# A two-layer decoder trunk on one core: the late modulation columns move from TensorE matmuls to VectorE dots

## The chip, the cores and the metric

The kernel runs on one core of a Trainium2 chip. The metric is the device time of one execution in microseconds (us). Three runs of the kernel before gave 1697.27, 1698.01 and 1699.43 us; their median, 1698.01 us, is the time that the change is measured against.

## The reference, cut to what matters

A trunk of two layers on `x` (1 x 1024 positions x 1024 channels, float32). Each layer computes

```
mod = c @ mod_w[layer] + mod_b[layer]          # c: 1 x 1024, mod_w[layer]: 1024 x 3072
shift, scale, gate = the three thirds of mod
h = rms_norm(x, norm_w[layer]) * (1 + scale) + shift
x = x + gate * mixer(h)
```

The mixer of layer 0 projects `h` to 2560 channels, which feed a causal convolution (with a layer norm behind it) and a state-space recurrence (with a GLU behind it), and projects the two branches back. The mixer of layer 1 is attention with rotary positions. The change concerns how 32 of the 48 blocks of 128 values of `mod` are computed: the gate of layer 0 and all of layer 1. Shift and scale of layer 0 are needed at once and are computed ahead of this stage by other code that stays as it is. The rest are the late columns.

## The kernel before, in words

Channels lie on the 128 partitions, positions on the free axis. A float32 product is made from three matmuls (high x high, low x high, high x low; `mm3`, lines 231 to 233), so every weight is split into a high and a low part: the high part on ScalarE (ACT, line 209), the low part on VectorE (DVE, line 212).

Layer 0 (`layer0`) is an order written out by hand: the order of the instructions on TensorE (PE), VectorE, ScalarE and, from the projections on, GpSimd (POOL) is that of the program. Only the order on SyncE (SP), which issues every DMA, is left to the scheduler. The loop that matters runs over half projections, t = 0 to 41: output block t // 2, position half t % 2, 24 matmuls of 128x512 each (12 for the GLU, t = 26 to 33). A step t puts into the queues, in this order: what takes the result of step t-1 out of PSUM (`evac`), at even t the split of the next weight (`begin`), the side work hung on this step with `at(t, ...)`, then `mod_turn` and `mod_step`, and last the matmuls of the half projection (names `p`, `pg`).

The side work is: the rotary angles (`rope_tables`, at step 1, 14 VectorE instructions of 128x512 on tiles `ro`, two ScalarE sines, two DMAs to DRAM); four quarters of the recurrence (`ssm_quarter`, quarter j at steps 4j+2 to 4j+11: tiles `pk`, `kp`, `pgt`, `T`, `sr`, `si`, `V`, `W`, `X`, `py`); four convolutions (`conv`, steps 4j+8 to 4j+12: `cm`, `pc`); the layer norm of the convolution in two halves b (`ln_sum`, `ln_mean`, `ln_center`, `ln_var`, `ln_rsqrt`, `ln_norm` at steps 27 + 4b to 31 + 4b: `mu`, `lq`, `va`). From step 42 the output projections follow (`o...` for positions of half 0, `p...` of half 1, tiles `poo`, `pop`), and beside those of half 1, at steps 57 to 60, `hidden(k)` makes the input of layer 1, two blocks k a step: `x` (line 217, VectorE), its high part (line 218, ScalarE), its low part on VectorE for even k (line 224) and on GpSimd for odd k (lines 226 and 227). At step 60 `open_slabs` puts the splits of layer 1's first four weights (`fr`) behind them on ScalarE and GpSimd.

The late columns are computed by `mod_rows` (lines 251 to 276), one generator step per half projection at t = 4 to 25, 27, 31, 34 to 41 and once behind the loop. The first of these steps issues three loads; each of the other 32 multiplies two of 64 chunks. A chunk is 128 input channels x 512 output columns of `mod_w` (`in_mod_r`, 256 KB), in three buffers (two in tile `mw`, one in the tile `cb`); four matmuls of 32 columns by 128 (line 272, tile `pr`) take the vector c, repeated over 32 columns, against it, and behind them the load into the same buffer is issued (line 259). Every eighth chunk ends a group of four blocks: ScalarE copies the rows (line 275), and in the next step `mod_turn` (lines 278 to 292) turns them into a column with one matmul (line 286, tile `mc`) and adds the bias on VectorE (line 288).

The dot that the change uses exists already: `dot_c` (line 238), used for the early scale columns, multiplies a tile by c, spread over all partitions in `cb`, and sums along the free axis.

PSUM has eight banks: tag `ps` 3 (half projections, `mc`), `pm` 2 (everything of the quarters and the layer norm), `pr` 1, `pc` 2.

Of the kernel before, what the change touches and what calls it, by code (L numbers as in the profile page):

```python
# [64 lines left out]

MODR = ((0, 16), (0, 20), (1, 8), (1, 12), (1, 0), (1, 4), (1, 16), (1, 20))


class Trunk:
# [180 lines left out]

    def mod_rows(self, ps, pr):

        nc = self.nc
        w = self.u("mw", tag="mw").rearrange("p (i m n) -> p i m n", i=2, m=4)
        w = [w[:, 0], w[:, 1], self.cb[:, 512:1024].rearrange("p (m n) -> p m n", m=4)]

        def load(c):
            if c < 8 * len(MODR):
                nc.sync.dma_start(w[c % 3], self.I["mod_r"][c // 8, c % 8])

        for c in range(3):
            load(c)
        crep = self.cb[:, 0:256].rearrange("p (k n) -> p k n", k=8)
        rows = self.cb[:, 256:384]
        p = pr("pr")[:, 0:128]
        for n, (layer, m) in enumerate(MODR):
            for q in range(4):
                yield
                for k in (2 * q, 2 * q + 1):
                    c = 8 * n + k  # L270
                    for j in range(4):
                        nc.tensor.matmul(p[32 * j:32 * j + 32], lhsT=crep[:, k], rhs=w[c % 3][:, j], start=(k == 0),
                                         stop=(k == 7), tile_position=(0, 32 * j))
                    load(c + 3)
            nc.scalar.activation(rows, p, AF.Copy)
            self.mod_late = (ps, rows, layer, m)

    def mod_turn(self):

        if self.mod_late is None:  # L280
            return
        ps, rows, layer, m = self.mod_late
        self.mod_late = None
        nc = self.nc
        c = ps(f"mc{layer}{m}")[:, 0:4]
        nc.tensor.matmul(c, lhsT=rows, rhs=self.ident[:, 0::32], start=True, stop=True)
        t = self.consts.tile([128, 4], F32, name=f"mod{layer}_{m}")
        nc.vector.tensor_tensor(t, c, self.mod_bias(layer, m, 4), op=ALU.add)
        self.mod[layer][m:m + 4] = [t[:, j:j + 1] for j in range(4)]
        if layer and 8 <= m < 16:  # L290
            nw = _cols()["norm_w"][0] + layer * 8 + m - 8
            nc.vector.scalar_tensor_tensor(self.g1[:, m - 8:m - 4], t, 1.0, self.pk[:, nw:nw + 4], ALU.add, ALU.mult)


    def layer0(self):
        nc, tc, I = self.nc, self.tc, self.I
        with self.cx0 as cx:
# [6 lines left out]
            def ps(name, shape=None, tag="ps"):  # L304
                return pp.tile(shape or [128, 512], F32, tag=tag, name=name, bufs={"ps": 3, "pm": 2}[tag])

            def pm(name, shape=None):
                return ps(name, shape, "pm")

            def pr(name):  # L310
                return pp.tile([128, 512], F32, tag="pr", name=name, bufs=1)

# [36 lines left out]
            with tc.tile_pool(name="start", bufs=8) as sp, order:  # L349
# [21 lines left out]
                def fetch_m(m):  # L371
                    mw[m] = sp.tile([128, 1024], F32, tag="m", name=f"mw0_{m}")
                    nc.sync.dma_start(mw[m], I["scale0"][m - 8] if m > 7 else I["shift0"][m])

# [77 lines left out]
                sh = pc("sh")  # L452
                pu, place = self.ssm_u_psum(ps, pm, pr)
                for k in range(8):
# [37 lines left out]
            nc.vector.tensor_copy(self.cb[:, 0:256].rearrange("p (k n) -> p k n", k=8),  # L492
                                  self.ccol.unsqueeze(2).to_broadcast([128, 8, 32]))
            cx.enter_context(tc.manual_schedule(engines={mybir.EngineType.DVE, mybir.EngineType.Activation,
# [37 lines left out]
            short = lambda a: a.rearrange("p (t c) -> p t c", t=8)  # L532
            mods = [None]
            self.mod_late = None

            def mod_step():
                if mods[0] is None:
                    mods[0] = self.mod_rows(ps, pr)
                next(mods[0], None)

# [7 lines left out]
            conv = [None] * 4  # L548
            at(1, self.rope_tables)
            for j in range(4):  # L550
# [66 lines left out]
            for b in range(2):  # L617
                at(25, ln_sum, b)
                t = 27 + 4 * b
                at(t, ln_mean, b)  # L620
                at(t, ln_center, b, 0)
                at(t + 1, ln_center, b, 1)
                at(t + 3, ln_var, b)
                at(t + 3, ln_rsqrt, b)
                at(t + 4, ln_norm, b, (0, 1, 2, 3))

# [67 lines left out]
            for t in range(42):  # L694
                i, h = divmod(t, 2)
                key = seq[i]
                if done:
                    evac(*done)
                if h == 0:
                    begin(i)  # L700
                for fn in side.pop(t, ()):
                    fn()
                self.mod_turn()
                if 4 <= t < 26 or t in (27, 31) or t > 33:
                    mod_step()
# [10 lines left out]
            mod_step()  # L716

# [36 lines left out]
            def hidden(k):  # L754
                h = self.h1[k][0] = self.u(f"h1_{k}_0", F32R, [128, 2, 512])
                self.affine(h[:, 0], h[:, 1], x0[k // 2][:, k % 2], self.g[1][k], st["r"], self.mod[1][k],
                            ("vector", "gpsimd")[k % 2])

# [5 lines left out]
            for k in range(8):  # L764
                at(57 + k // 2, hidden, k)
            at(60, open_slabs)
            done, po = None, {}
            for i in range(21, len(seq)):
                t, key = i + 21, seq[i]
                m, b = int(key[1]), int(key[0] == "p")  # L770
                if done:
                    residual(*done)
                    done = None
                begin(i)
                for fn in side.pop(t, ()):
                    fn()
                self.mod_turn()
# [12 lines left out]
                if key == "p0":  # L790
                    stat()
# [64 lines left out]
    def rope_tables(self):  # L856
        nc = self.nc
        xn = self.u("ro", shape=[128, 2, 8, 64], tag="mw")
        x, n = xn[:, 0], xn[:, 1]
# [651 lines left out]

    def ssm_u_psum(self, ps, pm, pr):
        p = {(j, h): (ps, ps, ps, pm, pm, pr)[2 * j + h](f"pu{j}_{h}") for j in range(3) for h in range(2)}
        mm = self.nc.tensor.matmul
# [23 lines left out]
    def ssm_quarter(self, j, us, ps, ysg):  # L1538
# [147 lines left out]
def lay_out(inp):  # L1686
    a = {k: np.asarray(v) for k, v in inp.items()}
    f = np.float32
# [8 lines left out]
    def put(name, v):  # L1697
# [51 lines left out]
        "ident": np.eye(128, dtype=f),  # L1749
        "scale0": a["mod_w"][0].T.reshape(24, 128, 1024)[8:16],  # L1750
        "mod_r": np.stack([a["mod_w"][i][:, 128 * m:128 * m + 512].reshape(8, 128, 512) for i, m in MODR]),
        "w0": tl(a["even_w_in"][0]).reshape(20, 128, 1024),
# [30 lines left out]
```

## Time and profile before

| | before |
|---|---|
| three runs, us | 1697.27, 1698.01, 1699.43 (median 1698.01) |
| the profiled execution, us | 1702.04 |
| its span, first to last instruction, us | 1700.3 |
| mean granted TensorE clock | 0.991 |
| TensorE busy | 1663.6 us (98%) |
| VectorE busy | 952.2 us (56%) |
| ScalarE busy | 618.9 us (36%) |
| GpSimd busy | 514.6 us (30%) |

Times in the rows are us from the start of the span unless they are marked ns. A matmul of float32 stands in the records as two, so `x8` are four instructions. The granted clock is a share of 2.4 GHz: 0.50 is 1.2 GHz. "Idle before, releaser" is the time that an engine sat still ahead of an instruction, and what ended it.

### The profile page before, as it was taken

The numbers are of one execution on the slowest core, as the hardware profiler recorded it, in microseconds if no ns is written. First come the engines' busy times: TensorE is split into PE (matmuls) and PEld (weight loads), VectorE is DVE, ScalarE is ACT, GpSimd is POOL, SyncE is SP. The second block draws the span as 40 slices with busy tenths as digits, with TensorE's granted clock in tenths as the row PEclk, the third lists the DMA queues.
The fourth block names the chain that finished last, engine by engine and source line by source line (L and its number), as shares of the span: only waits on it lengthen the run. The fifth ranks groups of instructions, "written<-read, shape, count | busy, mean of one in ns | idle before, by whom it ended". The sixth has DMA issues, their size and how long they took to land.

```text
span 1700.3 us, 28611 instructions
## 1 busy us (share of the span) xinstructions
PE 1663.6 (98%) x10520; PEld 1516.7 (89%) x10520; DVE 952.2 (56%) x2336; ACT 618.9 (36%) x1860; POOL 514.6 (30%) x733
## 2 busy tenths in 40 slices
PE   8989999999989999999999999999999999999999
PEld 5877777677769999999999999999999999999887
DVE  8964543545567446645654754754664575565541
ACT  5333333634344343333433334333333343333410
POOL 6454401000155323332332431432333233333000
PEclk9999999999989999999999999999999999999999
DMA  9355555346532012112112211211211211111252
GB/s 348 135 177 174 166 167 183 119 129 194 170 100 64 25 57 76 44 29 73 51 35 62 80 35 49 80 38 51 81 45 29 72 54 38 48 63 63 88 172 95
DMA packets 94189, 159.84 MB, mean 94 GB/s; under 512 B 13281, under 2 KB 43745, under 8 KB 94050
## 3 DMA queue, kind: packets, MB, share of 16 engines
q1 hardware_dynamic: 94050, 158.02, 30.0%
q8 instruction: 83, 1.36, 0.3%
q14 instruction: 56, 0.46, 0.1%
HBM read 130.54 MB, written 23.23 MB: 90 GB/s over the span
## 4 chain that ended last, share of the span: by engine, by line
PE 83%; issue 5%; DVE 4%; DMA 3%; ACT 2%; SPq 2%; POOL 1%; ACTq 0%; DVEq 0%; POOLq 0%
PE pj L231 17%; PE pj L233 17%; PE pj L232 17%; PE O L1149 4%; PE S L1100 4%; PE p L231 3%; PE p L232 3%; PE p L233 3%; PE tqk L1054 2%; PE tP L1127 2%; PE po L233 2%; PE po L232 2%; PE po L231 2%; DMA mw<-in_mod_r 1%; SPq L1669 1%
## 5 line engine op out<-in xcount | busy, mean ns | idle before, releaser
L231 PE MATMUL pj<-wh,h 128*128 128x384 f32 x1536 | 542.9, 353 | 0.0
L233 PE MATMUL pj<-wh,h 128*128 128x384 f32 x1536 | 516.7, 336 | 0.7 <-DVE h L224 0.7
L232 PE MATMUL pj<-wl,h 128*128 128x384 f32 x1536 | 516.0, 336 | 0.0
L231 PEld LDWEIGHTS pj<-wh,h 128*128 128x128 f32 x1536 | 289.1, 188 | 1.0 <-issue 0.2
L232 PEld LDWEIGHTS pj<-wl,h 128*128 128x128 f32 x1536 | 289.7, 189 | 0.3 <-issue 0.2
L233 PEld LDWEIGHTS pj<-wh,h 128*128 128x128 f32 x1536 | 288.3, 188 | 1.3 <-DVE h L224 1.3
L1039 POOL TENSOR_TENSOR B<-u,sin 128x256 f32<-128x256 f32 x192 | 190.1, 990 | 209.1 <-DVE u L1035 209.1
L1011 ACT ACTIVATE sq<-pj 128x128 f32<-128x128 f32 x384 | 103.0, 274 | 351.4 <-PE pj L233 317.9
L1012 POOL TENSOR_SCALAR ss<-ss 128x2 f32<-128x2 f32 x192 | 40.8, 212 | 488.4 <-ACT sq L1011 488.2
L212 DVE TENSOR_TENSOR wl<-raw,wh 128x768 fp32r<-128x768 f32 (+1 forms) x124 | 116.0, 950 | 124.2 <-ACT wh L209 123.6
L1035 DVE SCALAR_TENSOR_TENSOR u<-pj,ss,pk 128x128 f32<-128x128 f32 x384 | 116.4, 345 | 74.4 <-POOL ss L1013 74.2
L1076 DVE COPY qk<-tqk 128x256 f32<-128x256 f32 x188 | 79.2, 421 | 139.6 <-PE tqk L1054 139.6
L1013 POOL TENSOR_TENSOR ss<-ss,mh 128x2 f32<-128x2 f32 x192 | 139.1, 724 | 16.0
L1120 ACT ACTIVATE E<-E,nm 128x256 f32<-128x256 f32 (+2 forms) x128 | 71.3, 557 | 198.6 <-DVE nm L1119 198.6
L231 PE MATMUL p<-h0h,wh 128*128 128x512 f32 x272 | 113.1, 416 | 0.0
L233 PE MATMUL p<-h0h,wl 128*128 128x512 f32 x272 | 109.4, 402 | 0.0
L232 PE MATMUL p<-h0l,wh 128*128 128x512 f32 x272 | 109.3, 402 | 0.0
L209 ACT ACTIVATE wh<-raw 128x768 fp32r<-128x768 f32 (+1 forms) x124 | 97.3, 790 | 29.1 <-PE po L232 14.2
L1047 DVE TENSOR_TENSOR u<-A,B 128x128 f32<-128x128 f32 x192 | 56.2, 293 | 88.1 <-POOL B L1039 81.3
L1046 DVE TENSOR_TENSOR A<-u,cos 128x256 f32<-128x256 f32 x192 | 96.8, 504 | 4.4
L1100 PE MATMUL S<-qk 128*128 128x128 f32 x544 | 86.4, 274 | 0.0
L1100 PEld LDWEIGHTS S<-qk 128*128 128x128 f32 x544 | 80.9, 190 | 1.4
(452 smaller groups left out, 2797.3 us busy)
## 6 DMA issues: line engine op xcount, KB each, us to landing
raw<-in_wqkv SPq DMA_DIRECT2D x92, 384.0 KB
mw<-in_mod_r SPq DMA_DIRECT2D x43, 256.0 KB
wr<-in_w SPq DMA_DIRECT2D x17, 512.0 KB
al<-ad SPq DMA_DIRECT2D x16, 512.0 KB
cb<-in_mod_r SPq DMA_DIRECT2D x21, 256.0 KB
x<-in_x SPq DMA_DIRECT2D x8, 512.0 KB
mw<-in_scale SPq DMA_DIRECT2D x8, 512.0 KB
mw<-in_shift SPq DMA_DIRECT2D x8, 512.0 KB
```

Of the source, the lines that this page charges most:

```text
L209: nc.scalar.activation(hi, src, AF.Copy)
L212: getattr(nc, leng).tensor_tensor(lo, src, hi.bitcast(F32), op=ALU.subtract)
L231: mm(ps, lhsT=lh, rhs=rh, start=first, stop=False)
L232: mm(ps, lhsT=lh, rhs=rl, start=False, stop=False)
L233: mm(ps, lhsT=ll, rhs=rh, start=False, stop=last)
L1011: sc.activation(sq[:, i], p[:, i * 128:(i + 1) * 128], AF.Square, accum_out=ss[:, i:i + 1])
L1013: gp.tensor_tensor(ss, ss, mh, op=ALU.pow)
L1035: v.scalar_tensor_tensor(u[:, i].rearrange("p a b -> p (a b)"), p[:, i * 128:(i + 1) * 128], ss[:, i:i + 1], w, ALU.mult, ALU.mult)
L1039: gp.tensor_tensor(f(B), f(u), sin[:, ti].unsqueeze(1).to_broadcast([128, 4, 64]), op=ALU.mult)
L1046: v.tensor_tensor(f(A), f(u), cos[:, ti].unsqueeze(1).to_broadcast([128, 4, 64]), op=ALU.mult)
L1076: v.tensor_copy(out, tp)
L1100: pe.matmul(ps[:, i * 128:(i + 1) * 128], lhsT=qT[h, g, t], rhs=kT[h, g, kt], start=True, stop=True)
```

## The change

- `mod_rows` and `mod_turn` go, with the tile `pr`, its PSUM bank, the repeated c and the input `mod_r`. `mod_dots` comes: 64 dots, each over 128 output channels x 512 input channels of `mod_w` transposed (256 KB, 128 rows of 2 KB), behind each a load into its buffer (three buffers: two in `mw`, a new `mx`). Every eighth dot is followed by two adds of 128x4 (and for the scale of layer 1 one more instruction, as before).
- Two dots are put behind the matmuls of a half projection, at t = 4 to 26, 30 and 34 to 41. The first three loads are issued ahead of the loop.
- The rotary angles move from step 1 to step 20, into tiles of the pool `e`.
- The freed PSUM bank goes to `pm` (3 now). The tile `T` of the recurrence has one buffer instead of two.
- Layer norm: half 1 starts at step 30 instead of 31; the variance of half 0 comes at step 31 and its norm at 32 instead of 30 and 31. Variance and norm of half 1 stay at 34 and 35.
- `hidden(k)`: low parts on VectorE for all k, at steps 57, 58, 58, 59, 60, 60, 61, 62 instead of two each at 57 to 60.

```diff
-    def mod_rows(self, ps, pr):
...
-                for k in (2 * q, 2 * q + 1):
-                    c = 8 * n + k
-                    for j in range(4):
-                        nc.tensor.matmul(p[32 * j:32 * j + 32], lhsT=crep[:, k], rhs=w[c % 3][:, j], start=(k == 0),
-                                         stop=(k == 7), tile_position=(0, 32 * j))
-                    load(c + 3)
-            nc.scalar.activation(rows, p, AF.Copy)
...
+    def mod_dots(self):
...
+        w = self.u("mw", tag="mw")
+        w = [w[:, 0:512], w[:, 512:1024], self.c0.tile([128, 512], F32, name="mx")]
+        halves = [(layer, m, i) for layer, m0 in MODS for m in range(m0, m0 + 4) for i in range(2)]
...
+                nc.sync.dma_start(w[n % 3], self.I["mod_w"][layer, m][:, 512 * i:512 * i + 512])
+        for n in range(3):
+            load(n)
+        for n, (layer, m, i) in enumerate(halves):
+            yield
...
+            self.dot_c(h[:, n % 8 // 2, i:i + 1], w[n % 3], slice(512 * i, 512 * i + 512))
+            load(n + 3)
+            if n % 8 == 7:
...
+                nc.vector.tensor_tensor(t, h[:, :, 0], h[:, :, 1], op=ALU.add)
+                nc.vector.tensor_tensor(t, t, self.mod_bias(layer, m, 4), op=ALU.add)
...
-            at(1, self.rope_tables)
+            at(20, self.rope_tables)
...
-                t = 27 + 4 * b
+                t = 27 + 3 * b
...
-                at(t + 3, ln_var, b)
-                at(t + 3, ln_rsqrt, b)
-                at(t + 4, ln_norm, b, (0, 1, 2, 3))
+                at(t + 4, ln_var, b)
+                at(t + 4, ln_rsqrt, b)
+                at(t + 5, ln_norm, b, (0, 1, 2, 3))
...
-                self.mod_turn()
-                if 4 <= t < 26 or t in (27, 31) or t > 33:
-                    mod_step()
                 p = ps(f"p{key}_{h}")
...
                 done = (key, h, p)
+                if 4 <= t < 27 or t == 30 or t > 33:
+                    mod_step(2)
...
-                at(57 + k // 2, hidden, k)
+                at((57, 58, 58, 59, 60, 60, 61, 62)[k], hidden, k)
...
-        T = L(f"T{j}", "T", [128, 2, 4, 128], 2)
+        T = L(f"T{j}", "T", [128, 2, 4, 128])
```

## Rows read from the trace of the kernel before

**Rows 1.** The page: busy time of each engine; granted TensorE clock in 40 slices.
```profile
PE 1663.6 (98%) x10520; PEld 1516.7 (89%) x10520; DVE 952.2 (56%) x2336; ACT 618.9 (36%) x1860; POOL 514.6 (30%) x733
...
PEclk9999999999989999999999999999999999999999
```

**Rows 2.** What PE waited for, 0 to 560: total, times, longest.
```profile
PE pop L231 <- ACT whp L209: 4.7, 3, 3.7
PE pgt L1602 <- DVE kp L1589: 4.5, 1, 4.5
PE pr L272 <- DMA mw<-in_mod_r: 4.5, 5, 1.4
PE pop L233 <- DVE wlp L212: 4.0, 4, 2.5
PE va L605 <- DVE lq L599: 3.0, 1, 3.0
...
PE pr L272 <- DMA cb<-in_mod_r: 1.7, 1, 1.7
```

**Rows 3.** Stretches: length; busy PE, PEld, DVE, ACT, POOL (instructions); clock, DMA, GB/s.
```profile
96.00:389.00 293.00, 283.33 (x2410) 220.25 (x2408) 142.03 (x228) 112.89 (x161) 60.98 (x53) 0.98 0.51 155
95.00:100.00 5.00, 5.00 (x15) 4.04 (x15) 0.41 (x1) 0.60 (x1) 4.72 (x7) 0.50 0.99 298
178.00:221.00 43.00, 40.69 (x434) 32.27 (x426) 23.79 (x37) 14.67 (x20) 18.99 (x17) 0.96 0.55 168
221.00:260.00 39.00, 37.44 (x402) 29.66 (x402) 19.02 (x35) 13.33 (x18) 0.00 (x0) 1.00 0.61 182
...
336.00:340.00 4.00, 4.00 (x15) 3.13 (x12) 3.06 (x5) 2.21 (x3) 0.00 (x0) 0.62 0.76 212
```

**Rows 4.** PE in order of time (start, length): the first and the last late-column stretch.
```profile
110.89 0.64 PE L272 MATMUL pr<-mw,cb 128*32 128x128 f32 x16
111.47 0.50 PE L231 MATMUL p<-h0h,wh 128*128 128x512 f32 x1
...
388.06 0.42 PE L272 MATMUL pr<-cb 128*32 128x128 f32 x8
...
389.34 0.49 PE L231 MATMUL poo0b<-yc,who0b 128*128 128x512 f32 x1
```

**Rows 5.** PE in order of time: a matmul shortly behind a wait for a load.
```profile
193.06 0.63 PE L232 MATMUL p<-h0l,wh 128*128 128x512 f32 x1
```

**Rows 6.** VectorE: first and last rotary instruction; the longest form (min/median/max ns).
```profile
74.04 0.68 DVE L860 TENSOR_TENSOR ro<-posf,inv 128x512 f32<-128x512 f32 x1
...
88.58 1.39 DVE L183 TENSOR_SCALAR ro<-ro 128x512 f32<-128x512 f32 x1
...
L176 DVE SCALAR_TENSOR_TENSOR ro<-ro x6: 693/1174/1748, 76.9 to 83.6; 128x512 f32<-128x512 f32 x6
```

**Rows 7.** VectorE: the dot of the early columns (min/median/max ns) and its read-out.
```profile
L238 DVE CUSTOM_DVE_ANT_0 mw<-mw,cb x8: 1211/1220/1341, 16.7 to 61.0; 128x1024 f32<-128x1024 f32 x8
L238 DVE DVE_READ_ACCUMULATOR2_ANT mod<- x8: 76/82/89, 17.9 to 62.2; 128x1 f32 x8
```

**Rows 8.** VectorE at step 20 and PE at step 21: start, length, idle before.
```profile
256.44 1.22 DVE L212 TENSOR_TENSOR wl<-wr,wh 128x1024 fp32r<-128x1024 f32 x1 [8.73 <-ACT wh L209]
...
258.25 1.55 DVE L823 TENSOR_TENSOR cm<-csel,taps 128x640 f32<-128x640 f32 x2
...
266.07 2.38 PE L830 MATMUL pc<-Uc,cm 64*64 64x128 f32 x80
```

**Rows 9.** VectorE at step 58, and the low part for the last projection.
```profile
458.86 1.23 DVE L212 TENSOR_TENSOR wlp<-wrp,whp 128x1024 fp32r<-128x1024 f32 x1 [0.22 <-ACT whp L209]
460.00 1.78 DVE L217 SCALAR_TENSOR_TENSOR x<-x,g,rs 128x512 f32<-128x512 f32 x1
462.58 0.75 DVE L224 SCALAR_TENSOR_TENSOR h<-x,mod,h 128x512 fp32r<-128x512 f32 x1 [0.79 <-ACT h L218]
...
484.87 2.82 DVE L212 TENSOR_TENSOR wlp<-wrp,whp 128x1024 fp32r<-128x1024 f32 x1
```

More of the change, by code (lines that the diff above doesn't have):

```diff
@@ L62, in split_parts @@
     return out
-MODR = ((0, 16), (0, 20), (1, 8), (1, 12), (1, 0), (1, 4), (1, 16), (1, 20))
+MODS = ((0, 16), (0, 20), (1, 8), (1, 12), (1, 0), (1, 4), (1, 16), (1, 20))
 class Trunk:
@@ L249, in mod_bias @@
         return self.pk[:, o:o + n]
-    def mod_rows(self, ps, pr):
+    def mod_dots(self):
         nc = self.nc
[L254 to L268, printed above, removed]
-                for k in (2 * q, 2 * q + 1):
-                    c = 8 * n + k
-                    for j in range(4):
-                        nc.tensor.matmul(p[32 * j:32 * j + 32], lhsT=crep[:, k], rhs=w[c % 3][:, j], start=(k == 0),
-                                         stop=(k == 7), tile_position=(0, 32 * j))
-                    load(c + 3)
-            nc.scalar.activation(rows, p, AF.Copy)
-            self.mod_late = (ps, rows, layer, m)
@@ L278, in mod_turn @@
[L278 to L292, printed above, removed]
+        w = self.u("mw", tag="mw")
@@ new lines, in mod_dots, with load @@
+        w = [w[:, 0:512], w[:, 512:1024], self.c0.tile([128, 512], F32, name="mx")]
+        halves = [(layer, m, i) for layer, m0 in MODS for m in range(m0, m0 + 4) for i in range(2)]
+        def load(n):
+            if n < len(halves):
+                layer, m, i = halves[n]
+                nc.sync.dma_start(w[n % 3], self.I["mod_w"][layer, m][:, 512 * i:512 * i + 512])
[3 more added lines that the diff above has]
+            yield
+            if n % 8 == 0:
+                h = self.c0.tile([128, 4, 2], F32, tag="mh", name="mh", bufs=2)
+            self.dot_c(h[:, n % 8 // 2, i:i + 1], w[n % 3], slice(512 * i, 512 * i + 512))
+            load(n + 3)
+            if n % 8 == 7:
+                m -= 3
+                t = self.consts.tile([128, 4], F32, name=f"mod{layer}_{m}")
+                nc.vector.tensor_tensor(t, h[:, :, 0], h[:, :, 1], op=ALU.add)
+                nc.vector.tensor_tensor(t, t, self.mod_bias(layer, m, 4), op=ALU.add)
+                self.mod[layer][m:m + 4] = [t[:, j:j + 1] for j in range(4)]
+                if layer and 8 <= m < 16:
+                    nw = _cols()["norm_w"][0] + layer * 8 + m - 8
+                    nc.vector.scalar_tensor_tensor(self.g1[:, m - 8:m - 4], t, 1.0, self.pk[:, nw:nw + 4], ALU.add,
+                                                   ALU.mult)
@@ L304, in ps @@
             def ps(name, shape=None, tag="ps"):
-                return pp.tile(shape or [128, 512], F32, tag=tag, name=name, bufs={"ps": 3, "pm": 2}[tag])
+                return pp.tile(shape or [128, 512], F32, tag=tag, name=name, bufs=3)
             def pm(name, shape=None):
                 return ps(name, shape, "pm")
-            def pr(name):
-                return pp.tile([128, 512], F32, tag="pr", name=name, bufs=1)
             def pc(name):
@@ L372, in fetch_m @@
                     mw[m] = sp.tile([128, 1024], F32, tag="m", name=f"mw0_{m}")
-                    nc.sync.dma_start(mw[m], I["scale0"][m - 8] if m > 7 else I["shift0"][m])
+                    nc.sync.dma_start(mw[m], I["mod_w"][0, m] if m > 7 else I["shift0"][m])
                 def fetch_u(k):
@@ L452, in layer0 @@
                 sh = pc("sh")
-                pu, place = self.ssm_u_psum(ps, pm, pr)
+                pu, place = self.ssm_u_psum(ps, pm)
                 for k in range(8):
@@ L491, in layer0 @@
             self.ssm_params()
-            nc.vector.tensor_copy(self.cb[:, 0:256].rearrange("p (k n) -> p k n", k=8),
-                                  self.ccol.unsqueeze(2).to_broadcast([128, 8, 32]))
             cx.enter_context(tc.manual_schedule(engines={mybir.EngineType.DVE, mybir.EngineType.Activation,
@@ L532, in layer0, with mod_step @@
             short = lambda a: a.rearrange("p (t c) -> p t c", t=8)
[L533 to L539, printed above, removed]
+            mods = self.mod_dots()
+            next(mods)
+            def mod_step(n):
+                for _ in range(n):
+                    next(mods, None)
             side = {}
@@ L714, in layer0 @@
                 done = (key, h, p)
+                if 4 <= t < 27 or t == 30 or t > 33:
+                    mod_step(2)
             evac(*done)
-            mod_step()
             self.h1 = [[None, None] for _ in range(8)]
@@ L756, in hidden @@
                 self.affine(h[:, 0], h[:, 1], x0[k // 2][:, k % 2], self.g[1][k], st["r"], self.mod[1][k],
-                            ("vector", "gpsimd")[k % 2])
+                            "vector")
             def open_slabs():
@@ L776, in layer0 @@
                     fn()
-                self.mod_turn()
                 whole = len(key) == 2
@@ L857, in rope_tables @@
         nc = self.nc
-        xn = self.u("ro", shape=[128, 2, 8, 64], tag="mw")
-        x, n = xn[:, 0], xn[:, 1]
+        x, n = (self.ep.tile([128, 512], F32, tag="e", name=f"ro{i}").rearrange("p (a b) -> p a b", a=8)
+                for i in range(2))
         nc.vector.tensor_tensor(x, self.posf.unsqueeze(2).to_broadcast([128, 8, 64]),
@@ L1510, in ssm_params, with ssm_u_psum @@
         self.Kd = self.dram.tile([4, 128, 240], F32, name="Kd")
-    def ssm_u_psum(self, ps, pm, pr):
-        p = {(j, h): (ps, ps, ps, pm, pm, pr)[2 * j + h](f"pu{j}_{h}") for j in range(3) for h in range(2)}
+    def ssm_u_psum(self, ps, pm):
+        p = {(j, h): (ps if 2 * j + h < 3 else pm)(f"pu{j}_{h}") for j in range(3) for h in range(2)}
         mm = self.nc.tensor.matmul
@@ L1749, in lay_out @@
         "ident": np.eye(128, dtype=f),
-        "scale0": a["mod_w"][0].T.reshape(24, 128, 1024)[8:16],
-        "mod_r": np.stack([a["mod_w"][i][:, 128 * m:128 * m + 512].reshape(8, 128, 512) for i, m in MODR]),
+        "mod_w": a["mod_w"].transpose(0, 2, 1).reshape(2, 24, 128, 1024),
         "w0": tl(a["even_w_in"][0]).reshape(20, 128, 1024),
```

## The prediction

> **What bounds the kernel now.** I read the page first: TensorE (PE) is busy 98% of the span, VectorE 56%, and the granted clock is full but for two slices, the third and the twelfth [rows 1]. So time is won only by taking work or waits off PE, and VectorE has room on the average. Both dips of the clock lie in layer 0, the only part that the change touches. The list of what PE waited for shows why: 22 us of waits in six lines, on weights of the output projections, on `kp`, on loads of the late columns and on `lq` of the layer norm [rows 2]. The stretches give the room stage by stage: from step 4 to step 41 (96 to 389 us) PE is busy 283 of 293 us, VectorE 142, so VectorE is idle for 151 us [rows 3]. The order in time gives the price of the work that goes: between two half projections the late columns' matmuls stand alone, with nothing beside them on PE [rows 4].
>
> **The change part by part**, against the profiled execution (1702.0 us, 4.0 above the median of the runs).
>
> *The matmuls go.* The stretches are 32, one per pair of chunks. The first holds the next half projection back by 111.47 - 110.89 = 0.58 us, the last, with a transpose and a wait in it, by 1.28 [rows 4]. Read one by one they sum to 29.0 us: 32 x 0.57 = 18.2, waits for loads 4.5 + 1.7 = 6.2 [rows 2], the rest for eight transposes and restarts behind waits. All of it lies on PE's path. Ends: 18.2 if every wait comes back in another shape, 29.0 if none does. I take 29.0, since no instruction left on PE reads these loads.
>
> *A clock that fell with a wait.* Behind the longest of these waits, matmuls took 0.63 us [rows 5], the granted clock of 178 to 221 us is 0.96 [rows 3], and 43 x 0.04 = 1.7 us are lost there. They come back with the wait: +1.7 (0 to 1.7).
>
> *The rotary angles leave step 1.* They hold VectorE from 74.0 to 90.0 [rows 6]; `kp` stands behind them in its queue, and since `pm` has two banks, the second `pgt` waits 4.5 us for `kp` to be read [rows 2]. Behind it PE runs at 0.50, the 1.2 GHz level, from 95 to 100 [rows 3], another 2.5. With a third `pm` bank that transpose takes a free one, and `kp` comes 10 us earlier too; either removes the wait. +7.0 (4.5 to 7.0).
>
> *They arrive at step 20.* There they are queued between the split of a weight and the convolution's `cm`, for which PE's `pc` waits in step 21. The split starts at 256.4, `cm` at 258.3, its first half ends 0.8 later, and `pc` starts at 266.1 [rows 8], or at 265.5 without step 20's late columns. The 14 instructions took 15.9 us [rows 6], but beside a GpSimd that was nearly always busy; their longest form has 0.69 as its shortest and 1.75 as its longest time. From 221 to 260 GpSimd does nothing [rows 3], so I take about 8 (0.69 for the eight with two inputs, less for the six with one): 259.1 + 8 = 267.1, a new wait of 1.6 us. At 15.9 it would be 9.5; at the least, none. Two ScalarE sines and two DMAs go along; behind them on ScalarE stand the copies of `py`, whose banks are not wanted before step 27. -1.6.
>
> *The dots.* No dot of 512 is in the trace. One of 1024 takes 1.22 us and 0.08 for the read-out [rows 7]; by width that is 0.61 + 0.08, while instructions of 512 with two inputs take 0.69 at the least [rows 6]. I take 0.77 (0.69 to 1.30): 64 x 0.77 = 49 us (44 to 83), plus 16 small adds, 2 us, for the eight small adds and eight copies on ScalarE that go. This lies in 151 us of idle VectorE, beside PE, so its price is nothing but what it delays. The cover: a step of PE is 293 / 37 = 7.9 us on the average [rows 3] against 1.5 for two dots, a weight's split is wanted two steps later, PSUM of a half projection three steps later. Two places are tight. In the first quarter (steps 4 to 8) VectorE now carries eight dots, PE arrives 7 us earlier, and GpSimd is still busy (4.72 of 5 us at 95 to 100 [rows 3]): `X`, which `py` of step 8 needs, comes about when PE asks; -1.5 (0 to -5). And steps 26 to 35 hold the layer norm, where a late VectorE holds ScalarE's PSUM reads and the split for step 34: -1.5 (0 to -4.5).
>
> *The loads.* As many, of the same size, three buffers as before. But each waits in SP's queue for a dot instead of a matmul, with weights, recurrence and convolution transfers behind it. PE's waits for loads were 6.2 us in six [rows 2], 0.1 per chunk; the same on VectorE is 6 us of idle time. Nothing.
>
> *Layer norm.* Its second half is centred one step earlier while its variance stays at step 34, so the `va` wait of 3.0 [rows 2] goes, and with it the clock of 0.62 from 336 to 340 [rows 3], 1.5 us: +4.5 (0 to 4.5). Next in line is the split above.
>
> *`hidden`.* In the output projections VectorE sets the pace. A step with two blocks holds, besides residual and split, two `x`, a wait for ScalarE and a low part, among it 1.78 for an `x` that runs beside GpSimd. The last projection waits for ScalarE and then for a low part that ends at 484.9 + 2.8 = 487.7 [rows 9]; PE's waits for these weights are 8.7 us [rows 2]. In the new order I follow VectorE: residual and split take some 3.4 us a step by the lengths and waits of these rows, each block 2.1 (0.66, a wait of 0.79 for ScalarE, 0.66 [rows 9]). The split that now ends at 460.0 then ends at 459.2 (one block ahead of it, not two); steps of two, one and two blocks behind it give 466.9, 472.3 and, for the last, behind layer 1's four splits on ScalarE, 482 to 483.4: some 5 us earlier. I take +4.7 (0 to 8.7). The next to be late is that same weight.
>
> *Nothing:* one buffer for `T` (its next writer stands behind its last reader on VectorE anyway), the input's new name, a read of 2 KB rows as before.
>
> **Sum:** 29.0 + 1.7 + 7.0 + 4.5 + 4.7 = 46.9 gained, 1.6 + 1.5 + 1.5 = 4.6 lost: 42.3. The profiled execution would take 1659.7, the median **1656 us**. Layer 1 starts earlier by as much, and its PE stays busy, so nothing there absorbs it.
>
> **Rivals.**
>
> *VectorE late, waits come back (0.21).* For it: the order on VectorE is fixed, and one late instruction delays all behind it. Step 20 then costs 9.5 (+7.9), the first quarter 5 (+3.5), the waits of layer norm and last projection return (+4.5, +4.7): 1656 + 20.6 = 1677 us. Against it: half of VectorE's time is idle.
>
> *GpSimd shuts VectorE out (0.06).* The same form took 0.69 to 1.75 us while GpSimd was busy [rows 6]. GpSimd works 61 of 293 us in the dots' stage [rows 3], so 13 of 64 dots would take up to 1.06 more, 14 us on VectorE, of which only the first quarter's four, 4.2 us, reach PE: 1656 + 2.7 = 1659 us. The Trainium skill ("SBUF — State Buffer", section "Who interferes with whom") says that a VectorE instruction with two SBUF inputs and a GpSimd instruction that reads SBUF exclude each other for their whole length; a dot is such an instruction, so the page speaks against moving this work to VectorE, and the spread in the rows agrees with it.
>
> *All tight places hold (0.07).* The last projection gives all 8.7, and none of the 4.6 is lost: 1656 - 8.6 = 1647 us.
>
> *Slower: the loads pace VectorE (0.04).* The second dot of a step needs the load issued behind the first dot of the step before. If SP's queue is held, each dot stands waiting, with every PSUM read and split behind it. The stage then lasts 142 + 9 (angles) + 49 + 64 w for a wait w per dot, against 293 now, with 11.7 gained outside it: the kernel is slower from w = 1.64 us. At the longest wait of the rows, 1.7 [rows 2], it would be 142 + 9 + 49 + 109 = 309, that is 1702; longer waits cost 64 us for each us. Against it: the mean now is 0.1.
>
> **How the numbers follow.** The forecast as summed has 0.61, with its own range 1648 to 1666; the rest (0.01) is no change at all. Range: 1644 to 1678 takes in the forecast, the first three rivals and their bounds, and leaves out the slower case and the far ends. A measurement of this kernel can tell about 0.2%, 3.4 us, from no change. Faster by more: 0.94; within: 0.02; slower: 0.04.
>
> **What would show it.** Right: no wait on `kp` or `lq` in PE's list; clock 1.00 from 90 to 440 us; one half projection right behind the other where no side work stands; dots of 0.7 us; VectorE near 200 us busy where it was 142. Step 20: a wait of `pc` for `cm` of 1 to 2 us. Last projection: a low part 4 to 6 us earlier against the step before. Wrong: waits of PE for `X`, `wl` or a PSUM bank behind dots, VectorE waiting for `mw` by more than 0.5 us a dot, or layer 1 taking longer than before.

## The result, and the profile after

The changed kernel takes 1659.8 us (median of four runs, 1658.4 to 1663.7) where the kernel before took 1698.5 (median of four, 1697.3 to 1699.4): the ratio is 0.978, with a 95% interval of 0.976 to 0.980. The forecast was 1656 us in a range of 1644 to 1678. The profiled execution took 1658.4 us (span 1656.6), 43.6 less than that of before; the sum had said 42.3.

The page of the kernel after; its lines answer to [rows 1]:

```profile
PE 1632.3 (99%) x9992; PEld 1498.7 (90%) x9992; DVE 1005.1 (61%) x2475; ACT 615.1 (37%) x1851; POOL 502.2 (30%) x725
...
PEclk9999999999999999999999999999999999999999
```

PE lost 31 us of work, VectorE gained 53, and both dips of the clock are gone. What PE waited for, 0 to 520 us (total, times, longest), answers to [rows 2]:

```profile
PE pop L233 <- DVE wlp L212: 5.0, 4, 3.4
PE pop L231 <- ACT whp L209: 3.7, 1, 3.7
...
PE pc L809 <- DVE cm L802: 2.2, 1, 2.2
...
PE p L233 <- DVE wl L212: 0.5, 1, 0.5
```

The waits for `kp`, `lq` and for loads are gone. One for `cm` is new, and a small one for a split (`wl`). The two of the output projections are still there, with the same 8.7 us in total (5.0 + 3.7, and 4.7 + 4.0 in [rows 2]). The stretches that answer to [rows 3] (columns as there):

```profile
89.00:352.00 263.00, 260.06 (x1914) 208.51 (x1913) 212.48 (x383) 115.53 (x162) 70.21 (x56) 1.00 0.58 176
394.14:451.48 57.34, 48.52 (x195) 36.98 (x194) 35.38 (x41) 24.49 (x32) 7.59 (x4) 0.94 0.46 152
```

From the recurrence to the output projections PE now works 260.1 of 263 us at a clock of 1.00, with VectorE at 212.5. The second line is the tail of layer 0, from the first projection of the positions of half 1 (`p0`) to layer 1; there PE still stands for 8.8 us.

Totals of single executions differ by 2 us and more for one kernel, so the experiments are read by when PE starts the same work, in us from the start of the span (from the order in time on PE). A: first projection behind the first `pgt`. B: first projection behind the recurrence's first quarter. C: projection of step 21. D: step 34. E: first output projection. F: first matmul of layer 1.

| kernel | A | B | C | D | E | F | time |
|---|---|---|---|---|---|---|---|
| before | 95.50 | 111.47 | 269.27 | 336.11 | 389.34 | 495.13 | 1702.0 |
| after | 90.37 | 103.65 | 243.82 | 301.40 | 347.69 | 451.48 | 1658.4 |
| e1 | 93.18 | 106.46 | 244.93 | 302.52 | 348.81 | 455.08 | 1663.7 |
| e2 | 89.05 | 102.33 | 243.46 | 301.05 | 347.34 | 451.98 | 1659.0 |
| e3 | 93.09 | 106.36 | 245.65 | 303.25 | 349.63 | 455.50 | 1662.4 |
| e4 | 94.32 | 109.18 | 247.29 | 309.13 | 356.16 | 461.96 | 1670.5 |
| e5 | 90.36 | 103.65 | 241.88 | 299.46 | 345.77 | 450.55 | 1657.6 |
| e6 | 94.28 | 108.86 | 246.72 | 304.31 | 350.61 | 455.22 | 1662.1 |
| e7 | 89.39 | 102.52 | 261.74 | 325.14 | 374.44 | 487.98 | 1694.9 |
| e8 | 89.63 | 102.96 | 244.83 | 302.65 | 348.79 | 452.57 | 1660.0 |
| e9 | 90.14 | 103.42 | 245.22 | 308.22 | 354.38 | 457.21 | 1665.1 |
| e10 | 89.86 | 103.14 | 244.58 | 302.56 | 348.88 | 455.45 | 1664.0 |
| e11 | 89.42 | 102.69 | 244.47 | 302.09 | 348.41 | 446.41 | 1661.7 |
| e12 | 90.52 | 103.81 | 242.05 | 299.64 | 345.93 | 446.81 | 1655.4 |

The gain at F is 495.13 - 451.48 = 43.65, all that the two executions differ by: layer 1 takes 1205 us in both.

### The profile page after: what moved, and what is told of

It reads as the page before. It is cut to its first block, busy times and chain, and to the rows that moved or that the text cites. A ratio compares the mean times of both kernels' runs of the same rounds, so it can differ in the third digit from the quotient of the medians.

```text
span 1656.6 us, 27694 instructions
## 1 busy us (share of the span) xinstructions
PE 1632.3 (99%) x9992; PEld 1498.7 (90%) x9992; DVE 1005.1 (61%) x2475; ACT 615.1 (37%) x1851; POOL 502.2 (30%) x725
## 4 chain that ended last, share of the span: by engine, by line
PE 91%; DVE 3%; ACT 2%; issue 1%; POOL 1%; DMA 1%; SPq 0%; DVEq 0%; ACTq 0%; POOLq 0%
PE pj L231 18%; PE pj L233 18%; PE pj L232 17%; PE O L1128 4%; PE S L1079 4%; PE p L231 4%; PE p L233 4%; PE p L232 4%; PE tqk L1033 3%; PE tP L1106 2%; PE po L233 2%; PE po L231 2%; PE po L232 2%; PE pc L809 1%; PE pu L1500 1%
## 5 line engine op out<-in xcount | busy, mean ns | idle before, releaser
L990 ACT ACTIVATE sq<-pj 128x128 f32<-128x128 f32 x384 | 102.6, 273 | 351.6 <-PE pj L233 325.2
L231 PE MATMUL p<-h0h,wh 128*128 128x512 f32 x272 | 109.5, 402 | 0.2 <-ACT gs L672 0.2
```

Source lines behind the costliest of these rows:

```text
L231: mm(ps, lhsT=lh, rhs=rh, start=first, stop=False)
L990: sc.activation(sq[:, i], p[:, i * 128:(i + 1) * 128], AF.Square, accum_out=ss[:, i:i + 1])
```

## The experiments

**e1, e2, e3: the two moves that may have removed the wait for `kp`.** e1 puts the rotary angles back, e2 the PSUM banks, e3 both.

```
-            at(20, self.rope_tables)
+            at(1, self.rope_tables)                         (e1, e3)
-  bufs=3
+  bufs={"ps": 3, "pm": 2, "pr": 1}[tag]                     (e2, e3)
```

e1. 

> The kernel after with the rotary angles back in step 1; the third pm bank stays. If the bank is what removed the wait for kp, no wait for kp shows in PE's list, and the 2.2 us wait of pc for cm behind step 20's angles is gone too: milestone 'end of step 20's projection' unchanged (239.3 us), layer 1's first matmul some 2 us earlier than the 451.5 of the change. If kp's place in VectorE's queue is what counts, a wait of some 4.5 us and a half-speed clock (2.5 us) return at 90 to 100 us, and layer 1 starts some 5 us later.

e2. 

> The kernel after with PSUM as before (two pm banks, a pr bank that only one pu tile uses); the angles stay at step 20. If either of the two moves alone removes the wait for kp, as the prediction says, nothing changes by 100 us (third phase starts at 90.4, the first projection behind it at 103.7). Rival: the third bank did it, and the second pgt waits 2 to 5 us for kp. Later on, with two banks for pm, a wait of up to 1 us per use could show where pm tiles follow closely; I expect layer 1's first matmul within 1.5 us of 451.5.

e3. 

> Both undone: angles in step 1 and two pm banks. Both theories: the wait for kp of 4.5 us and the clock at its lower level behind it come back, so the milestone at the first projection behind the recurrence's first quarter comes some 7 us later than 103.7; pc's wait for cm goes (2.2 gained). Layer 1's first matmul 4 to 5 us later than 451.5. If it comes back by less than 5 us at 103.7, the term of 7.0 in the sum was another thing.

e2 came out as expected: no wait for `kp`, A and B 1.3 us earlier than in the kernel after (the first phase ended so much sooner), and a wait of 0.8 for the second quarter's `pk`, which the kernel after doesn't have. In e1 and e3 no wait for `kp` came back either, though both theories had expected one in e3. The reason is in VectorE's order. The first rotary instruction in e3:

```profile
39.94 1.21 DVE L839 TENSOR_TENSOR ro<-posf,inv 128x512 f32<-128x512 f32 x1
```

With the scratch that the change gives them (tiles that are free early) the angles of step 1 run from 39.9 us on, among the blocks of the first phase, instead of at 74.0 as in [rows 6]. The first phase is 2.8 us longer for it (A: 93.18 against 90.37), and `kp` is early. So e1 and e3 didn't test the place of before; e5 and e6 do.

**e4: the matmuls alone, with their transposes and loads, leave the kernel before.** The late columns are the bias alone. In `mod_rows` (cut):

```
-  nc.sync.dma_start(w[c % 3], self.I["mod_r"][c // 8, c % 8])
...
-  nc.tensor.matmul(p[32 * j:32 * j + 32], lhsT=crep[:, k], rhs=w[c % 3][:, j], ...)
...
-  self.mod_late = (ps, rows, layer, m)
+  t = self.consts.tile([128, 4], F32, name=f"mod{layer}_{m}")
+  nc.vector.tensor_copy(t, self.mod_bias(layer, m, 4))
```

> The kernel before with the late columns' matmuls, transposes and loads left out (the columns are then the bias alone), all else in its old place. If the main term is right as 29.0 + 1.7 us, this kernel takes 30 to 31 us less than the kernel before on the same chip, and the waits for kp (4.5), lq (3.0) and in the last projection stay. Rival: the waits for loads come back behind something else, and only 18 to 25 us are gained; or other waits go as well (VectorE and SP freed) and over 33 us are gained.

At F it is 495.13 - 461.96 = 33.2 us ahead of the kernel before. Of that 1.2 was there at A already; from A to F it is 32.0, against 30.7 in the sum. The other waits stay, as expected; its list of PE's waits:

```profile
PE pgt L1587 <- DVE kp L1574: 4.5, 1, 4.5
PE va L590 <- DVE lq L584: 3.8, 1, 3.8
```

So the late columns' matmuls gave 32 us from A to F, and the rest of the change 10.5 (461.96 - 451.48). By whole times e4 gained less than the 30 to 31 us expected: 1670.5 against 1699.0 for the kernel before on the same chip, 28.5, one run each. Of the 4.7 us between this and the 33.2 at F, 1.6 were lost in layer 1, which took 1206.7 us here; by the other 3.1 the kernel before ran faster there than in its profiled execution (1702.0).

**e5, e6: the angles in step 1, held there by their scratch.** e5 with three `pm` banks, e6 with two.

```
-  x, n = (self.ep.tile([128, 512], F32, tag="e", ...) ...)
+  xn = self.sp.tile([128, 2, 4, 128], F32, tag="T", name="ro") ...
-  at(20, self.rope_tables)
+  at(1, self.rope_tables)
```

e5. 

> The kernel after with the rotary angles back in step 1, their scratch taken from T's buffer so that they can't run ahead of the first phase, as they did in the first two experiments. The third pm bank stays, VectorE's order at step 1 is that of the kernel before. Bank theory: the second pgt takes a free bank, no wait for kp, first projection behind the first quarter at 103 to 104.5 us. Queue theory: kp is late again and the wait of some 4.5 us with 2.5 us of lower clock is back: 110 to 111. pc's wait for cm (2.2) goes in either case.

e6. 

> As the one before, with two pm banks: both moves undone, VectorE's order at step 1 as in the kernel before. Expected: the wait of PE for kp (4.5 us) and the lower clock behind it are back, the first projection behind the first quarter comes 6.5 to 7.5 us later than in the kernel after. If it isn't back, the term of 7.0 belongs to neither move but to another edit.

PE in e5 and then in e6 (order in time: start, length, idle before):

```profile
89.58 1.03 PE L1581 MATMUL pgt<-ident,G 128*128 128x128 f32 x8
```

```profile
90.29 0.60 PE L1581 MATMUL pgt<-ident,G 128*128 128x128 f32 x4
93.61 1.01 PE L1581 MATMUL pgt<-ident,G 128*128 128x128 f32 x4 [2.73 <-DVE kp L1568]
```

The stretch from 95 to 100 us, in e5 and then in e6 (columns as in [rows 3]):

```profile
95.00:100.00 5.00, 5.00 (x24) 4.03 (x23) 2.09 (x3) 1.55 (x2) 4.72 (x6) 1.00 0.76 227
```

```profile
95.00:100.00 5.00, 5.00 (x19) 3.99 (x18) 0.00 (x0) 0.26 (x1) 4.72 (x7) 0.79 0.81 258
```

VectorE writes `kp` at 92.6 us in e5 and at 93.2 in e6, as late in the one as in the other. With a third bank the eight transposes go through; with two, four of them wait, and the clock behind them falls. The bank theory holds: B is 103.65 in e5 and 108.86 in e6. The 5.2 us are 0.7 of a later start, the wait, and the lower clock; 4.5 without the start, less than the 6.5 expected. The scratch held the angles less well than meant: the first three ran from 65.8 us on in e6, among the weight splits ahead of step 1, so `kp` came 1.1 us earlier than before (93.2 against 94.3), and PE asked for it 0.7 later. Together with e2 this shows that either move alone removes the wait for `kp`, and that both together buy nothing more there. In e5 PE has no wait for `cm` any more, and C comes 243.82 - 241.88 = 1.9 us sooner than after.

**e7, e8: the dots twice, and not at all.** In e8 the late columns are the bias alone.

```
   self.dot_c(h[:, n % 8 // 2, i:i + 1], w[n % 3], ...)
+  self.dot_c(h[:, 4, 0:1], w[n % 3], ...)                   (e7)
-  self.dot_c(h[:, n % 8 // 2, i:i + 1], w[n % 3], ...)      (e8)
-  load(n + 3)                                               (e8)
```

e7. 

> The kernel after with every 512-wide dot done twice (the second into a spare column, same order, same loads): 64 x 0.77 = 49 us more on VectorE. If dots are free as long as VectorE has idle time, the price is what exceeds it: from 102 to 240 us VectorE was busy 124.5 of 138, and some 17 steps bring 26 us more into 13.5 us of room, so layer 1's first matmul comes 10 to 20 us later than 451.5. Rival, every dot is on the path: 49 us later. Rival, VectorE has more room than the busy times say: under 5 us later.

e8. 

> The kernel after with the 64 dots and their loads left out (the late columns are the bias alone), all else as in the change: the price that dots and loads have on PE's path. My reading of the trace: first quarter nothing, layer norm about 1 us, so layer 1's first matmul 0 to 2 us earlier than 451.5, pc's wait for cm still about 2. Rival: the dots delay step 20 and the last projections too, 4 us or more earlier.

The stage in e8 and in e7 (columns as above):

```profile
89.00:352.00 263.00, 260.11 (x1907) 208.66 (x1905) 158.50 (x247) 115.00 (x160) 66.42 (x55) 0.99 0.39 117
```

```profile
89.00:375.00 286.00, 266.71 (x1893) 213.06 (x1892) 244.45 (x482) 110.09 (x150) 69.76 (x55) 0.95 0.54 158
```

Without the dots VectorE is busy 54 us less, and PE's work is the same to 0.05 us: from B to step 20's projection PE takes 130.0 us without dots (102.96 to 232.97) and 129.8 with them (103.65 to 233.45). The dots cost PE nothing. F itself isn't 0 to 2 us earlier in e8, as expected, but 1.1 later, because `pc` of step 21 ran there at a lower clock (last section). A second set of 64 holds VectorE for 45 us more (line 238: 102.6 us in all against 57.2) and costs 36.5 us at F (487.98 - 451.48), far over the 10 to 20 expected. VectorE is busy 244 of 286 us there, so its mean would still leave room; PE's waits in e7 say where there is none:

```profile
PE py L1644 <- DVE X L1631: 9.7, 3, 4.5
PE poo1b L231 <- ACT who1b L209: 4.9, 1, 4.9
...
PE va L588 <- DVE lq L582: 2.5, 1, 2.5
PE poo1b L233 <- DVE wlo1b L212: 2.4, 1, 2.4
```

My expectation set 26 us of dots against 13.5 of idle time in one stretch and counted no lower clock. The waits come in lumps: `py` three times, the layer norm, and the first output weights, whose splits stand behind the dots. Behind the longer of them the clock falls (0.50 at 208 to 214 us and at 382 to 388; 0.95 over the stage).

**e9: the layer norm at its old steps.**

```
-  t = 27 + 3 * b
+  t = 27 + 4 * b
   (variance and scale at t + 3, the normalized blocks at t + 4)
```

> The kernel after with the layer norm's steps as in the kernel before (second half centred at step 31, variance at step 34). My sum gave this edit 4.5 us: the wait of va for lq of 3.0 us and a lower clock behind it (1.5). Expected: the wait is back, step 34's projection starts 3 to 4.5 us later than the 301.4 us of the kernel after. Rival: VectorE, freed or loaded by the other edits, has lq ready in time, and nothing changes at 301.4; or the wait is longer, over 5 us, since dots now stand ahead of lq.

PE and VectorE in e9 (order in time):

```profile
307.18 2.02 PE L587 MATMUL va<-lq,ones 128*128 128x512 f32 x2 [4.84 <-DVE lq L581]
```

```profile
303.25 1.23 DVE L212 TENSOR_TENSOR wl<-wr,wh 128x1024 fp32r<-128x1024 f32 x1 [0.25 <-ACT wh L209]
304.40 1.28 DVE L578 SCALAR_TENSOR_TENSOR cv<-mu,cv 128x512 f32<-128x512 f32 x2
306.44 0.69 DVE L581 TENSOR_TENSOR lq<-lq,lq 128x512 f32<-128x512 f32 x1 [0.76 <-ACT lq L580]
```

The wait is back, and longer than the 3.0 of [rows 2]. From the start of step 33's projection (296.97 after, 298.60 in e9) to D it is 4.4 us after and 9.6 in e9: the edit is worth 5.2, more than the 4.5 at most that was expected. The last dot ahead of `lq` ends 12 us before it, and e4, which has no dots, shows 3.8 of the same wait; that the dots lengthen it isn't shown, and what does stays open.

**e10: the old order of `hidden`.**

```
-  at((57, 58, 58, 59, 60, 60, 61, 62)[k], hidden, k)
+  at(57 + k // 2, hidden, k)
   (every second block's low part on GpSimd)
```

> The kernel after with hidden as before: two blocks at each of steps 57 to 60, every second one with its low part on GpSimd. By the two traces the tail (from the output projections' p0 to layer 1's first matmul) got 2.0 us shorter; my sum said 4.7. If the new order of hidden did that, layer 1's first matmul comes 1.5 to 2.5 us later than 451.5 (step 53's projections on), with waits for whp and wlp in the middle projections as in the kernel before. If it did more and something else took it back (four splits of layer 1's first slabs on ScalarE), 4 us or more later. If it did nothing, under 0.7 us.

F comes 4.0 us later, but E was 1.2 late already; from p0 to F it is 59.3 us (396.17 to 455.45) against 57.3 after (394.14 to 451.48): 1.9, the size that the first theory expected. Its cause is another, though. The same stretch in e10, in the kernel before and in e1, whose tail is that of the kernel after (columns as in [rows 3]):

```profile
396.17:455.45 59.28, 50.26 (x195) 38.08 (x194) 35.35 (x37) 24.11 (x32) 23.04 (x12) 0.91 0.47 150
```

```profile
436.51:495.13 58.62, 49.85 (x196) 37.64 (x194) 35.36 (x37) 24.06 (x32) 23.02 (x12) 0.91 0.47 152
```

```profile
396.32:455.08 58.76, 50.21 (x196) 38.05 (x194) 35.07 (x41) 24.49 (x32) 7.58 (x4) 0.91 0.46 150
```

PE stands still for 9.0 us in e10 (59.28 - 50.26), 8.8 before and 8.8 after. What differs is the clock, 0.91 against 0.94 in the kernel after, and e1 has the 0.91, and 58.8 us, with the new order of `hidden` too. At the same clock the old order costs 0.5 us (e10 against e1); the other 1.4 are the clock of one execution.

**e11: layer 1's first slabs one step later.**

```
-  at(60, open_slabs)
+  at(61, open_slabs)
```

> The kernel after with the opening of layer 1's slabs (their loads and four splits on ScalarE) one step later, behind the split of the last projection's weight. My theory: those four splits hold the last weight's split, so that PE waits 3.7 us for whp and 3.4 us for wlp in the last projection. Expected: both waits fall to under 1 us each, layer 1's first matmul 5 to 7 us earlier than 451.5, unless layer 1 then waits for its slabs. Rival: the last split is late because VectorE and GpSimd are late, and the waits stay within 1 us of what they are.

F comes 5.1 us earlier, and 5.8 against E. But the next list shows what took the place of the two waits:

```profile
PE st L945 <- DVE xq L720: 7.0, 1, 7.0
...
PE pop L233 <- DVE wlp L212: 2.1, 4, 0.5
PE pop L231 <- ACT whp L209: 1.9, 2, 1.3
```

ScalarE, VectorE and GpSimd in e11 (order in time):

```profile
444.24 2.77 ACT L209 ACTIVATE wh<-fr 128x768 fp32r<-128x768 f32 x3 [0.56 <-DMA fr<-in_wqkv]
446.91 0.62 ACT L719 ACTIVATE xq<-x 128x512 f32<-128x512 f32 x1
```

```profile
447.56 2.20 DVE L720 TENSOR_TENSOR xq<-xq,xq 128x512 f32<-128x512 f32 x1 [3.49 <-ACT xq L719]
```

```profile
443.76 7.65 POOL L212 TENSOR_TENSOR wl<-fr,wh 128x768 fp32r<-128x768 f32 x4 [169.81 <-DMA fr<-in_wqkv]
```

The four splits were what held the last weight, as the theory had it: without them ahead, and without GpSimd beside it, its low part takes 1.23 us where it takes 2.82 in the kernel after. One step later they hold the squares (`xq`) instead, for whose sum layer 1 waits 7.0 us, and 30 us into layer 1 the kernel is 3.3 us behind the kernel after. The stall had only moved.

**e12: both cures.** Angles in step 1 as in e5, slabs opened at step 55 and split two by two at steps 56 and 57.

```
-  at(60, open_slabs)
+  at(55, open_slabs)
+  for k in range(4):
+      at(56 + k // 2, lambda: next(slabs, None))
```

> The kernel after with two edits: the rotary angles in step 1 as in the fifth experiment (no wait of pc for cm), and layer 1's first slabs opened at step 55 instead of 60, their four splits two each at steps 56 and 57, while ScalarE and GpSimd have room and before the blocks of hidden need VectorE. Theory: the last projection's 3.7 + 3.4 us go, and, unlike with slabs at step 61, the last square and its sum are not behind the splits either, so nothing takes their place: layer 1's first matmul at 443 to 446 instead of 451.5, median 5 to 8 us below the change (1652 to 1655). Rival: the splits at steps 56 and 57 hold the projections there (waits for whp and wlp of 2 us or more each), and the gain is under 3 us. Rival: the pace of the tail is VectorE's, not the splits', and p7 waits as before.

Five runs have a median of 1655.0 us, the upper end of what was expected; the ratio to the kernel before is 0.9735 (0.9722 to 0.9749), below that of the change. PE's waits from 380 to 520 us:

```profile
PE pop L233 <- DVE wlp L212: 2.9, 4, 1.3
PE pop L231 <- ACT whp L209: 2.5, 2, 1.4
...
PE st L955 <- DVE xq L720: 1.2, 1, 1.2
```

The last projection's 7.0 us are 1.6 (1.1 for its high part, 0.5 for its low part). The longest waits of this list stand elsewhere: 1.3 for `wlp` at step 59 and 1.4 for `whp` at step 60. F lies at 446.8, just outside the 443 to 446 expected. The projections at steps 60 and 61 start 2.8 us and 1.4 us later against the one before them than in the kernel after, the first for these two waits, the second for the clock behind them (0.79 from 425.6 to 433.6). So the first rival holds in part, with its waits three steps later than it said: of the 4.7 us gained at F, 0.9 are those of the angles (e5), and 3.7 are left for the slabs.

## Why the prediction was right, and where it was not

| term of the sum | forecast | measured | from |
|---|---|---|---|
| matmuls, and the clock behind a load wait | 30.7 | 32.0 | e4 against before, A to F |
| `kp` and the clock behind it | 7.0 | 7.2 | before against after at B: 7.82, less one stretch of 0.58 |
| angles at step 20 | -1.6 | -1.9 | after against e5, B to C |
| first quarter | -1.5 | 0 | after against e8, B to step 20 |
| layer norm | 4.5 - 1.5 | 3.6 - 0.5 | start of step 33's projection to D: 8.60 before, less 0.58 for a stretch, less 4.43 after; then the wait for `wl` |
| tail | 4.7 | 2.0, by luck | E to F: 105.79 before, 103.79 after; see below |
| sum | 42.3 | 42.4 | 43.65 at F |

**The matmuls** went as the sum had it; that no instruction left on PE reads these loads was enough. **The wait for `kp`** went for the reason given, and "either removes the wait" is now shown for each move by itself (e2, e5), with the wait back when both are undone (e6). The way was longer than "`kp` stands behind them in its queue", though. ScalarE and then VectorE in the kernel before:

```profile
88.58 0.63 ACT L184 ACTIVATE ro<-ro 128x512 f32<-128x512 f32 x1 [12.94 <-DVE ro L182]
```

```profile
92.59 1.82 DVE L212 TENSOR_TENSOR wl<-wr,wh 128x1024 fp32r<-128x1024 f32 x1 [2.61 <-ACT wh L209]
94.33 0.28 DVE L1589 COPY kp<-pk 128x128 f32<-128x128 f32 x1
```

ScalarE held the next weight's high part behind the two sines, and these waited for the angles; VectorE, done with the angles at 90.0, then waited for that weight. Without the angles `kp` comes at 87.15, 7.2 us earlier and not the 10 said. That was enough.

**The angles at step 20** are the new wait that the forecast named. VectorE behind the weight's split, and PE, answer to [rows 8]:

```profile
231.32 0.69 DVE L839 TENSOR_TENSOR ro<-posf,inv 128x512 f32<-128x512 f32 x1
...
239.43 0.43 DVE L183 TENSOR_SCALAR ro<-ro 128x512 f32<-128x512 f32 x1
...
240.44 1.55 DVE L802 TENSOR_TENSOR cm<-csel,taps 128x640 f32<-128x640 f32 x2
```

```profile
241.51 2.38 PE L809 MATMUL pc<-Uc,cm 64*64 64x128 f32 x80 [2.22 <-DVE cm L802]
```

They take 8.5 us (8 said), and PE waits 2.2 (1.6 said). What the sum left out is the clock behind such a wait, which some executions show (below).

**The dots** took 0.69 us each where nothing was beside them, with a read-out of 0.08. All dots of the kernel after, the eight early ones of 1024 included (min/median/max ns), and VectorE's idle time for their loads:

```profile
L238 DVE DVE_READ_ACCUMULATOR2_ANT mh<- x64: 75/81/85, 105.9 to 349.3; 128x1 f32 x64
L238 DVE CUSTOM_DVE_ANT_0 mw<-mw,cb x51: 666/687/1859, 16.8 to 348.7; 128x512 f32<-128x512 f32 x43, 128x1024 f32<-128x1024 f32 x8
L238 DVE CUSTOM_DVE_ANT_0 mx<-mx,cb x21: 678/685/1815, 111.8 to 348.0; 128x512 f32<-128x512 f32 x21
...
  DMA mw<-in_mod_w: 6.8, 6
  DMA mx<-in_mod_w: 1.7, 1
```

14 of the 64 ran beside GpSimd's `TENSOR_TENSOR` work and took 1.59 to 1.86, where the rival on GpSimd said 13; the lock that it was made of is there. With them the dots hold VectorE for 57 us, not the 49 of the estimate. The Trainium skill ("SBUF — State Buffer", section "Who interferes with whom") says that two-input VectorE work and GpSimd's reads shut each other out, and the trace agrees. But none of it reached PE: in the first quarter, where the rival put 4.2 us, PE has no wait, and e8 shows nothing to win. VectorE stood 6.6 us for loads in these 64 dots (the other 1.9 of the 8.5 belong to the early ones), 0.10 each, against the 1.64 from which the slower case decides. The cover has an end, as e7 shows: a second set costs PE four fifths of its own length.

**The layer norm** gave what was said in the balance, 3.1 against 3.0: at D 3.6 of the 4.5, and behind D the split that was feared late costs 0.5 instead of 1.5. It isn't the dots that make it late: e8, which has none, shows the same 0.5.

**The tail is the step that failed.** The text had the last weight's low part done "some 5 us earlier" in a term of 4.7, and asked for it "4 to 6 us earlier against the step before". From the start of step 61's projection to PE's first use of that low part it was 14.0 us before (473.75 to 487.75) and is 14.4 after (430.41 to 444.78). ScalarE and VectorE in the kernel after; the second answers to the last of [rows 9]:

```profile
435.14 0.83 ACT L209 ACTIVATE wh<-fr 128x768 fp32r<-128x768 f32 x1
436.41 2.75 ACT L209 ACTIVATE wh<-fr 128x768 fp32r<-128x768 f32 x3 [0.43 <-DMA fr<-in_wqkv]
439.06 0.61 ACT L719 ACTIVATE xq<-x 128x512 f32<-128x512 f32 x1
439.58 1.04 ACT L209 ACTIVATE whp<-wrp 128x1024 fp32r<-128x1024 f32 x1
```

```profile
441.91 2.82 DVE L212 TENSOR_TENSOR wlp<-wrp,whp 128x1024 fp32r<-128x1024 f32 x1
```

The new order of `hidden` did speed VectorE up at the steps ahead: the waits for `whp` at steps 60 and 61 are gone (0.2 and 0.8 us before). But the last weight doesn't hang on it. Four splits and a wait for their load stand ahead of `whp` on ScalarE, and their low parts on GpSimd stretch `wlp` to the same 2.82 us as before; PE's last wait for it grew from 2.5 to 3.4 us. In total the waits for these weights are 8.7 us as before, so the term of 4.7 came to nothing. I had the splits in the chain and credited the faster VectorE with time that only moving the splits gives (e11, e12).

The 2.0 us that the table shows for the tail are luck of the two executions: 1.3 from p0 to F are the clock (0.91 before, 0.94 after, with PE idle for 8.8 us in both), and 0.7 ahead of p0 is mostly a wait of 0.9 for `who3a`, which e1, e2 and e5 have too, with the tail of the kernel after. Without them the sum is 40.4, not 42.4.

**The median** came out 3.8 us above the forecast though the profiled gain was 1.3 above the sum. The step from the one to the other took the profiled execution to lie 4.0 above the median, as before the change. After it, the profiled execution lies 1.4 below its median. By the medians the change gained some 39 us and not 43.6, so the table, which compares these two executions, fits the sum better than the kernels do. The clock goes with this difference: nine runs of the kernel before beside e12 have mean clocks from 0.993 (1698.0 us) to 0.991 (1702.5), and the profiled one had 0.991; the four of the kernel after go from 0.996 (1658.4) to 0.993 (1663.7).

## What to carry to other kernels

Work moved to an engine off the path is free as long as each consumer's margin in steps holds, which the engine's mean load doesn't tell: here 54 us cost nothing and the next 45 cost 36. Before a stall is booked as gained, follow the last instruction that it waits for on every engine that feeds it; a pace that improves elsewhere doesn't pay there. Before a difference of 1 to 2 us between two executions is given to an edit, compare PE's idle time and its clock in that stretch: e10's 1.9 us looked like a confirmed forecast and were mostly clock. When an operation is put back for a test, look at where it ran: a new scratch buffer moved the angles 34 us ahead of their step.

## What the runs showed of the hardware

PE's clock after one and the same short wait differs from execution to execution. Seven kernels have the wait of 2.2 to 2.3 us for `cm` at step 21. Behind it the small matmuls of `pc` (80 records) took 2.38 us in the kernel after, in e2 and in e7, and 3.64 to 3.98 in e8 to e11, though e9 to e11 change nothing ahead of step 27. In e8 (order in time, and the stretch of 243 to 246 us):

```profile
241.02 3.88 PE L804 MATMUL pc<-Uc,cm 64*64 64x128 f32 x80 [2.19 <-DVE cm L797]
```

```profile
243.00:246.00 3.00, 3.00 (x42) 2.50 (x37) 1.49 (x2) 0.00 (x0) 0.00 (x0) 0.65 0.40 85
```

A mean of 0.65 says that PE was at its lower level, 1.2 GHz, for most of these 3 us; in the kernel after the clock is 1.00 there. From the start of this `pc` to that of the next it is 8.1 us after and 9.7 in e8 to e11. A wait of 2.2 us therefore costs 2.2 us or 3.8, and one profiled execution shows only one of the two. The tail shows the same: from p0 to F the kernel after and e1 run the same code with 8.8 and 8.6 us of waits, and e1 takes 1.4 us longer at its lower clock. The Trainium skill ("TensorE: Matmul & The Clock Gate", section "Part 1: The HAM clock gate (the "warmup" mystery)") says of the start of a kernel that the number of slow matmuls varies from run to run of the same kernel; here it varies in the middle of one too.
